# Relative-position bias and softmax: reloads moved to GpSimd's queue, stores to SyncE's, four rows to a chunk

One core of one Trainium2 chip (trn2) runs the kernel. The metric is the time of one execution in device microseconds (us), smaller is better.

## The reference, cut to what matters

```python
def reference(logits, rel_bias):          # logits [2, 8, 2112, 2112] f32, rel_bias [8, 33]
    rel = clip(pos[:, None] - pos[None, :], -16, 16) + 16
    logits = logits + rel_bias[:, rel][None]
    exp = np.exp(logits - logits.max(axis=-1, keepdims=True))
    return exp / exp.sum(axis=-1, keepdims=True)
```

285.5 MB are read and as much is written; each element gets one addition, one exponential and one multiplication.

## The kernel before

Each of 128 partitions owns 264 rows of 2112 elements (8448 bytes). A chunk is 3 rows of every partition, so 88 chunks pass through 8 buffers in SBUF, in place. `F` holds the bias as one strip per partition, built at the start from a small table.

```python
    R = 3                                   # rows of a partition in one chunk
    PARTS = [(0, 2), (2, R)]                # adds and exponentials go in these pieces
    BUFS = 8
    N = T // R                              # 88 chunks
    ...
    def take(eng, sem, v):
        eng.wait_ge(sem, v).then_inc(sem, -v)
    def load(eng, u, start):
        eng.dma_start(out=L[u][:], in_=rows(logits, start)).then_inc(loaded[u], 16)
    def reload(eng, u, start):
        take(eng, stored[u], 16)            # the buffer's store has landed
        load(eng, u, start)
    ...
        @block.sync                         # SyncE: every load
            for c0, c1 in FIRST: ...        # first chunk: four quarter rows, then two rows
            for u in range(1, BUFS):
                if u == BUFS - 1:
                    take(eng, made, 1)      # the last buffer is scratch until the strip is made
                load(eng, u, u * R)
            passes(eng, BUFS, N - 1, lambda u, start: reload(eng, u, start))
        @block.scalar                       # ScalarE: exponentials, and every store
            def whole(u, start):
                exps(eng, u)
                store(eng, u, start)        # waits until VectorE has scaled the chunk
        @block.vector                       # VectorE: the strip, then for each chunk
            ...                             #   bias add, reciprocal of the sums, scaling
```

The softmax here doesn't subtract the row's maximum and nothing guards it: scores larger than these inputs give would overflow.

## Time and profile before

| | before |
|---|---|
| median of 3 runs | 1332.85 us (1332.46 to 1333.08) |
| span of the profiled run | 1331.0 us |
| VectorE, ScalarE busy | 73%, 39% |
| bytes moved, mean rate | 571.0 MB, 429 GB/s |
| DMA packets | 26,501 |
| a load lands after, a store after | 65.9 us, 39.9 us |

To read it: when two transfer queues together fill the DMA engines for nearly the whole span, the time is the bytes plus what is lost at the two ends. The engines' own idle time is then only a consequence. "Lands after" is the median time from the issue of a transfer to its completion; much of it is waiting behind transfers queued earlier.

### The profile page before, as it was taken

The page shows a single profiled execution, that of the slowest core. Times are in us where ns is not written, and L with a number is a line of the kernel's source. Part 1 is how long each engine was busy: PE and PEld are TensorE (multiplying, and loading weights), DVE is VectorE, ACT ScalarE, POOL GpSimd, SP SyncE. Part 2 cuts the span into 40 slices and gives each one's busy share as a digit, 9 for nine tenths or more (in the row PEclk, how much of TensorE's full clock was granted, in tenths as well). Part 3 has the DMA queues.
Part 4 walks back from the last instruction along what each step waited for, and adds up shares of the span by engine and source line. Part 5 has one row for each costly group of instructions (what it writes and reads, how often), then busy time and mean ns, then how long its engine had stood idle before and what let it go on. Part 6 is the DMA issues. An engine that isn't in the chain of part 4 may idle for free. (4 is left out here: it accounts for less than half of the span.)

```text
span 1331.0 us, 3010 instructions
## 1 busy us (share of the span) xinstructions
DVE 968.3 (73%) x627; ACT 524.8 (39%) x529; POOL 0.5 (0%) x6
## 2 busy tenths in 40 slices
DVE  6787867777677777677677777777676776777774
ACT  2535344334433344334433344333443344333441
POOL 0000000000000000000000000000000000000000
DMA  9999999999999999999999999999999999999998
GB/s 374 436 429 436 428 437 428 436 430 436 430 436 429 436 429 436 429 436 430 434 431 434 431 434 431 434 431 433 432 433 431 434 431 434 431 433 431 433 432 347
DMA packets 26501, 571.02 MB, mean 429 GB/s; under 512 B 3072, under 2 KB 3072, under 8 KB 3584
## 3 DMA queue, kind: packets, MB, share of 16 engines
q1 hardware_dynamic: 13536, 285.48, 50.0%
q10 hardware_dynamic: 12960, 285.50, 49.8%
q14 instruction: 5, 0.04, 0.0%
HBM read 285.49 MB, written 285.47 MB: 429 GB/s over the span
## 5 line engine op out<-in xcount | busy, mean ns | idle before, releaser
L125 ACT ACTIVATE L<-L 128x2112 f32<-128x2112 f32 x264 | 515.2, 1952 | 770.3 <-ACTq L88 770.3
L116 DVE TENSOR_TENSOR L<-L,F 128x4224 f32<-128x4224 f32 (+1 forms) x176 | 600.8, 3455 | 137.8 <-DVEq L88 137.7
L143 DVE TENSOR_SCALAR L<-L,tot 128x2112 f32<-128x2112 f32 x264 | 340.5, 1318 | 28.2 <-DVEq L88 6.2
L139 DVE RECIPROCAL tot<-tot 128x2 f32<-128x2 f32 (+1 forms) x176 | 28.3, 161 | 175.5 <-DVEq L88 175.5
L125 ACT ACTIVATION_READ_ACCUMULATOR L<-L 128x1 f32 x264 | 49.2, 186 | 0.0
L125 ACT ACT_TABLE_LOAD x1 | 1.3, 1283 | 18.9 <-ACTq L88 18.9
L187 DVE TENSOR_SCALAR L<-L,rbP 128x71 f32<-128x71 f32 x1 | 0.3, 258 | 3.4 <-DVEq L88 3.4
L195 DVE TENSOR_TENSOR F<-L,rbP 128x2343 f32<-128x2343 f32 x1 | 2.6, 2601 | 0.1
L196 DVE TENSOR_TENSOR F<-F,L 128x2343 f32<-128x2343 f32 x1 | 2.6, 2600 | 0.1
L182 DVE TENSOR_SCALAR L<-L 128x71 int32<-128x71 int32 x1 | 0.2, 198 | 1.5 <-DVEq L88 1.5
L185 DVE TENSOR_SCALAR L<-L 128x71 f32<-128x71 f32 x3 | 0.6, 198 | 0.5 <-DVEq L88 0.2
L190 DVE SCALAR_TENSOR_TENSOR L<-L,rbP 128x71 f32<-128x71 f32 x1 | 0.3, 295 | 0.2 <-DVEq L88 0.2
L183 DVE TENSOR_TENSOR L<-L 128x71 f32<-128x71 int32 x1 | 0.2, 235 | 0.1
L188 DVE COPY F<-rbP 128x16 f32<-128x16 f32 x1 | 0.2, 175 | 0.1
L194 DVE COPY F<-rbP 128x16 f32<-128x16 f32 x1 | 0.2, 174 | 0.1
L246 POOL IOTA L<- 128x71 int32 x1 | 0.2, 189 | 0.0
L243 POOL IOTA L<- 128x71 int32 x1 | 0.2, 188 | 0.6 <-SPq L74 0.6
L290 POOL MEMSET const-uint8-127<- 128x1 uint8 x1 | 0.1, 103 | 0.0
L290 POOL MEMSET const-bfloat16-1.0<- 128x1 bf16 x1 | 0.1, 102 | 0.0
L290 POOL MEMSET const-float32-0.0<- 128x1 f32 x1 | 0.1, 99 | 0.2 <-issue 0.2
L290 POOL MEMSET const-float32-1.0<- 128x1 f32 x1 | 0.1, 98 | 0.0
## 6 DMA issues: line engine op xcount, KB each, us to landing
out_dram<-L ACTq DMA_DIRECT2D x87, 3168.0 KB, 39.9
L<-in_logits_dram SPq DMA_DIRECT2D x86, 3168.0 KB, 65.9
L<-in_logits_dram SPq DMA_DIRECT2D x3, 1056.0 KB, 10.0
L<-in_logits_dram SPq DMA_DIRECT2D x1, 2112.0 KB, 63.2
out_dram<-L ACTq DMA_DIRECT2D x1, 2112.0 KB, 9.6
L<-in_logits_dram SPq DMA_DIRECT2D x4, 264.0 KB, 3.5
out_dram<-L ACTq DMA_DIRECT2D x1, 1056.0 KB, 13.5
rbP<-in_rel_bias_dram ACTq DMA_DIRECT2D x2, 8.2 KB
```

The lines of the kernel that those rows point to most:

```text
L116: eng.tensor_tensor(out=x3, in0=x3, in1=F3, op=ALU.add).then_inc(added, 1)
L125: e = eng.activation(out=x, in_=x, func=EXP, accum_out=tot[u][:, i : i + 1])
L139: eng.reciprocal(out=t, in_=t).then_inc(inverted, 1)
L143: e = eng.tensor_scalar_mul(out=x, in0=x, scalar1=tot[u][:, i : i + 1])
L182: step(eng.tensor_single_scalar(out=qi, in_=qi, scalar=M * Q - 1, op=ALU.bitwise_and))
L183: step(eng.tensor_tensor(out=qm, in0=qi, in1=mm, op=ALU.subtract))
L185: step(eng.tensor_scalar(out=m, in0=qm, scalar1=0.0, scalar2=None, op0=op))
L187: step(eng.tensor_scalar(out=rest, in0=lt, scalar1=low, scalar2=None, op0=ALU.mult))
L190: eng.scalar_tensor_tensor(out=rest, in0=gt, scalar=high, in1=rest, op0=ALU.mult, op1=ALU.add)
L195: step(eng.tensor_tensor(out=blocks, in0=wide(eq), in1=rev, op=ALU.mult))
L196: step(eng.tensor_tensor(out=blocks, in0=blocks, in1=wide(rest), op=ALU.add))
L290: nc = _bacc.Bacc("TRN2", target_bir_lowering=False, num_devices=1)
```

## The change

Its intent: let an otherwise idle engine issue the reloads, take the stores' waits out of ScalarE's stream, make transfers larger, and bring the first chunk in whole rows. The core of the diff:

```diff
-    R = 3
+    R = 4
-    BUFS = 8
+    BUFS = 6
...
         @block.sync
-            for c0, c1 in FIRST: ...
+            for r0, sem in ((0, loaded[0]), (1, late)):   # rows 0 and 2, then rows 1 and 3
+                ...
             for u in range(1, BUFS):
-                load(eng, u, u * R)
-            passes(eng, BUFS, N - 1, lambda u, start: reload(eng, u, start))
+                load(eng, u, u * R, loaded[u])
+            passes(eng, 0, N - 1, lambda u, start, loads: store(eng, u, start))
...
         @block.gpsimd
+            passes(eng, BUFS, N - 1, lambda u, start, loads: reload(eng, u, start))
...
         @block.scalar
-            whole(0, 0)
-            passes(eng, 1, N - 3, whole)
+            exps(eng, 0)
+            passes(eng, 1, N, lambda u, start, loads: exps(eng, u))
```

(Reloads count on semaphores of their own that only grow, so the loops pass the value to wait for; the last chunk is loaded and stored in two pieces.)

More of the change, by code (lines that the diff above doesn't have):

```diff
@@ L64 @@
     mm = mm.bitcast(INT32)
-    FIRST = [(S * m // 4, S * (m + 1) // 4) for m in range(4)]
-    FIRST += [(S * m, S * (m + 1)) for m in range(1, R)]
     def rows(t, start, run=RS):
@@ L75 @@
     loaded = [nc.alloc_semaphore(f"loaded{u}") for u in range(BUFS)]
+    reloaded = [nc.alloc_semaphore(f"reloaded{u}") for u in range(BUFS)]
     stored = [nc.alloc_semaphore(f"stored{u}") for u in range(BUFS)]
@@ L80 @@
     late = nc.alloc_semaphore("late")
+    last = nc.alloc_semaphore("last")
     made = nc.alloc_semaphore("made")
@@ L88, in take, with load @@
         eng.wait_ge(sem, v).then_inc(sem, -v)
-    def load(eng, u, start):
-        eng.dma_start(out=L[u][:], in_=rows(logits, start)).then_inc(loaded[u], 16)
+    def load(eng, u, start, sem):
+        eng.dma_start(out=L[u][:], in_=rows(logits, start)).then_inc(sem, 16)
     def store(eng, u, start, r0=0, r1=R):
@@ L100, in reload @@
         take(eng, stored[u], 16)
-        load(eng, u, start)
+        load(eng, u, start, reloaded[u])
     def add(eng, u, r0, r1, start):
@@ L116, in add, with exps @@
         eng.tensor_tensor(out=x3, in0=x3, in1=F3, op=ALU.add).then_inc(added, 1)
-    def exps(eng, u, first=None):
+    def exps(eng, u):
         for r0, r1 in PARTS:
             take(eng, added, 1)
-            if first and r0 == 0:
-                first()
             for i in range(r0, r1):
@@ L126, in exps, with vec @@
             e.then_inc(summed, 1)
-    def vec(eng, u, start, parts=()):
-        if not parts:
-            take(eng, loaded[u], 16)
-        for m, (r0, r1) in enumerate(PARTS):
-            if parts:
-                take(eng, parts[m], 16)
+    def vec(eng, u, start, loads, parts=False):
+        for (r0, r1), load in zip(PARTS, loads):
+            if load:
+                eng.wait_ge(*load)
             add(eng, u, r0, r1, start)
@@ L147, in passes @@
     def passes(eng, n0, n1, body):
-        k = (n1 - n0) // BUFS * BUFS
-        with eng.Fori(n0 * R, (n0 + k - BUFS) * R + 1, BUFS * R) as i:
-            for u in range(BUFS):
-                body((n0 + u) % BUFS, i + u * R)
-        for n in range(n0 + k, n1):
-            body(n % BUFS, n * R)
+        k = (n1 - n0) // BUFS
+        with eng.Fori(0, (k - 1) * 8 + 1, 8) as i:
+            for m in range(BUFS):
+                n = n0 + m
+                body(n % BUFS, i * (BUFS * R // 8) + n * R, i * 2 + 16 * (n // BUFS))
+        for n in range(n0 + k * BUFS, n1):
+            body(n % BUFS, n * R, 16 * (n // BUFS))
     def strip_of(eng):
@@ L213, in _ @@
         def _(eng):
-            for c0, c1 in FIRST:
+            for r0, sem in ((0, loaded[0]), (1, late)):
+                m = (R - r0 + 1) // 2
+                x = L[0]
                 eng.dma_start(
-                    out=L[0][:, c0:c1],
+                    out=bass.AP(
+                        tensor=x.tensor,
+                        offset=x.offset + r0 * S,
+                        ap=[[list(x.ap[0])[0], P], [2 * S, m], [1, S]],
+                    ),
                     in_=bass.AP(
                         tensor=logits.tensor,
-                        offset=logits.offset + c0,
-                        ap=[[T * S, P], [1, c1 - c0]],
+                        offset=logits.offset + r0 * S,
+                        ap=[[T * S, P], [2 * S, m], [1, S]],
                     ),
-                ).then_inc(loaded[0], 16)
+                ).then_inc(sem, 16)
             for u in range(1, BUFS):
@@ L227, in _ @@
                     take(eng, made, 1)
-                load(eng, u, u * R)
-            passes(eng, BUFS, N - 1, lambda u, start: reload(eng, u, start))
+                load(eng, u, u * R, loaded[u])
+            passes(eng, 0, N - 1, lambda u, start, loads: store(eng, u, start))
             u = (N - 1) % BUFS
-            take(eng, stored[u], 16)
-            for (r0, r1), sem in zip(PARTS, (loaded[u], late)):
-                eng.dma_start(
-                    out=L[u][:, r0 * S : r1 * S],
-                    in_=rows(logits, (N - 1) * R + r0, (r1 - r0) * S),
-                ).then_inc(sem, 16)
+            for r0, r1 in PARTS:
+                store(eng, u, (N - 1) * R, r0, r1)
             for n in range(N - BUFS, N - 1):
@@ L248, in _ @@
             )
+            passes(eng, BUFS, N - 1, lambda u, start, loads: reload(eng, u, start))
+            u = (N - 1) % BUFS
+            take(eng, stored[u], 16)
+            for (r0, r1), sem in zip(PARTS, (reloaded[u], last)):
+                eng.dma_start(
+                    out=L[u][:, r0 * S : r1 * S],
+                    in_=rows(logits, (N - 1) * R + r0, (r1 - r0) * S),
+                ).then_inc(sem, 16)
         @block.scalar
@@ L252, in _ @@
             table_load(eng, range(B))
-            def whole(u, start):
-                exps(eng, u)
-                store(eng, u, start)
-            whole(0, 0)
-            passes(eng, 1, N - 3, whole)
-            u = (N - 3) % BUFS
-            exps(eng, u)
-            exps(eng, (N - 2) % BUFS, lambda: store(eng, u, (N - 3) * R))
-            store(eng, (N - 2) % BUFS, (N - 2) * R)
-            exps(eng, (N - 1) % BUFS)
-            for r0, r1 in PARTS:
-                store(eng, (N - 1) % BUFS, (N - 1) * R, r0, r1)
+            exps(eng, 0)
+            passes(eng, 1, N, lambda u, start, loads: exps(eng, u))
         @block.vector
@@ L271, in _ @@
             strip_of(eng)
-            eng.wait_ge(loaded[0], 16 * len(FIRST)).then_inc(loaded[0], 16 - 16 * len(FIRST))
-            passes(eng, 0, N - 1, lambda u, start: vec(eng, u, start))
+            take(eng, late, 16)
+            for u in range(BUFS):
+                vec(eng, u, u * R, [(loaded[u], 16), None])
+            passes(
+                eng,
+                BUFS,
+                N - 1,
+                lambda u, start, loads: vec(eng, u, start, [(reloaded[u], loads), None]),
+            )
             u = (N - 1) % BUFS
-            vec(eng, u, (N - 1) * R, parts=(loaded[u], late))
+            whole = 16 * ((N - 1) // BUFS)
+            vec(eng, u, (N - 1) * R, [(reloaded[u], whole), (last, 16)], parts=True)
 _INS = ['logits', 'rel_bias']
```

## The prediction

> **What bounds the kernel now.** I began with the page, parts 1 to 3, to see who is full.
>
> ```profile
> span 1331.0 us, 3010 instructions
> DVE 968.3 (73%) x627; ACT 524.8 (39%) x529; POOL 0.5 (0%) x6
> ...
> DMA  9999999999999999999999999999999999999998
> ...
> q1 hardware_dynamic: 13536, 285.48, 50.0%
> q10 hardware_dynamic: 12960, 285.50, 49.8%
> ```
>
> VectorE is at 73%, ScalarE at 39%, while the DMA engines stand at nine tenths or more in all but the last slice. The two queues of part 3, loads (q1, issued by SyncE) and stores (q10, by ScalarE), fill 50.0 + 49.8 = 99.8% of sixteen engines' span. No engine instruction can be the bound; the bytes are.
>
> Next I asked whether the compute engines' waits point the same way (the view of waits, SyncE's queue first: engine and line, what it waited for, us in total, times, longest), and what the DMA queues hold (part 6 of the page: KB each, us from issue to landing):
>
> ```profile
> SPq L88 <- SPq L88: 1276.8, 89, 34.7
> ACT L L125 <- ACTq L88: 770.3, 88, 9.5
> DVE L L116 <- DVEq L88: 137.7, 77, 4.5
> ...
> out_dram<-L ACTq DMA_DIRECT2D x87, 3168.0 KB, 39.9
> L<-in_logits_dram SPq DMA_DIRECT2D x86, 3168.0 KB, 65.9
> ```
>
> VectorE waits 77 times ahead of its bias add, mostly for a load: it is fed, not feeding. A load lands 65.9 us after its issue and a store after 39.9 us. A chunk is 3168 KB each way, so at 432 GB/s a load and a store of it take 2 x 3.244 MB / 432 GB/s = 15.0 us. The 105.8 us in the two queues are thus seven chunk times: there is always work queued. With the 14.6 us from a load's use to its store (VectorE's first add at 14.23 us, the store at 28.87 us) the ring closes: 105.8 + 14.6 = 120.4 = 8 buffers x 15.05 us.
>
> Last, the windows of the two ends, as a saturated kernel can lose time only there (columns: busy time of VectorE, ScalarE, GpSimd, clock, DMA share, GB/s):
>
> ```profile
> 0.00:10.00 10.00, 3.85 (x10) 0.00 (x0) 0.53 (x6) 1.00 0.77 266
> 200.00:600.00 400.00, 292.55 (x187) 156.09 (x158) 0.00 (x0) 1.00 1.00 433
> 1310.00:1320.00 10.00, 5.80 (x6) 2.06 (x2) 0.00 (x0) 1.00 1.00 432
> 1320.00:1331.00 11.00, 0.00 (x0) 0.00 (x0) 0.00 (x0) 1.00 0.42 178
> ```
>
> Against 433 GB/s the first 10 us lose 10 x (433 - 266) / 433 = 3.9 us and the last 11 lose 11 x (433 - 178) / 433 = 6.5 us. Nothing is lost between.
>
> The trace's DMA records give the cost of one descriptor on one engine, the same in both directions: a median 319 ns for 8,448 bytes, 629 ns for 16,896, 940 ns for 25,344. The slope is (940 - 319) ns / 16,896 B, or 27.2 GB/s an engine; what remains is 319 - 310.5 = **8.5 ns for each descriptor**. A completion write takes 9 ns. A chunk gives each engine 8 descriptors (128 partitions over 16 engines), so before needs 88 chunks x 2 x 8 x 940 ns = 1323.5 us of an engine. The span's other 7.5 us are 2.2 us until bytes flow, slow first pieces, completion writes, and a tail in which some engines finish after others.
>
> **What the Trainium skill says.** "DMA: Bandwidth & Descriptors", section "Specifications", puts the ceiling at 435 GB/s, 27.2 for an engine; the slope agrees exactly, and the middle's 433 leaves little. The same page, "Issuing engines are not separate DMA queues", says that DMAs from sync, scalar and gpsimd run on the same 16 engines, so another issuer saves issue time only. An issue here takes 0.34 us (SyncE and ScalarE), 0.34 of each 15 us, and hidden: no gain. "Queues, rings and completion order" says that an engine takes a queue's descriptors in ring order and goes round robin between queues; the equal halves of q1 and q10 fit. "SBUF — State Buffer", section "SBUF: two separate sides", warns that GpSimd writes its descriptors through a port pair that VectorE's two-port operations lock. VectorE's scaling of a row (tensor_scalar, 1318 ns) is about half of a row's add (4.55 us for two), so it does run in such a mode; the kernel before issues no DMA from GpSimd, so the stall itself is in no trace yet.
>
> **The change part by part.**
> 1. *Four rows a chunk.* 66 chunks instead of 88. A descriptor of 33,792 bytes is an estimate from the slope: 1242 + 8.5 = 1250.5 ns. Each engine does 66 x 2 x 8 x 1250.5 ns = 1320.5 us, **3.0 us less**. Completion writes per engine go from 94 loads and 89 stores to 68 and 67: 48 x 9 ns = **0.4 us less**.
> 2. *First and last chunk in pieces.* The first becomes two transfers of whole rows, 512 descriptors of 8,448 bytes where 128 would do: 384 x 8.5 ns / 16 = 0.2 us more. The last in halves, both ways: 0.14 us more. The quarter rows of before go (105 ns on average against 86 typical, 512 of them: 0.6 us), but 512 whole rows at 342 against 319 ns on average bring 0.7 back. Sum: **0.3 us more**.
> 3. *VectorE's work* is the same rows in fewer instructions. One chunk is two adds of 4.55, then the second pair of exponentials (4.15 us from the second add's end to the reciprocal, as in the timeline), a reciprocal and two scalings of 2.85 together: 16.2 us, of a new chunk time of 20.06 us. Before it was 13.15 of 15.05. Slack grows from 1.9 to 3.8 us a chunk. Off the path both times: 0.
> 4. *Stores in SyncE's queue behind its first loads.* The first six chunks, 26 MB, take about 60 us at 436 GB/s. The first store can be issued near 31 us but its descriptors stand behind the loads in the ring, so it runs from about 62 us and the first reload follows at about 72 us (before: 49.1). The engines stay full all the while: loads to 62 us, then stores 0 and 1, already computed. 0 on the time, but the queues change places: with each reload issued as a store ends, about one load is in flight and four stores are queued. The total in both queues should be 6 x 20.06 - 17 = 103 us, now some 20 to 30 us for a load and 75 to 85 for a store.
> 5. *GpSimd as issuer.* 61 reload transfers. A stall behind two scalings (2.6 us) plus some 1 us of generation delays a reload by up to 4 us, while the store queue keeps the engines full: nothing on the path; I allow 0.5 us.
> 6. *The tail.* From the last load to the last store's issue is 11.6 us (add 4.55, exponentials 4.15, scaling 2.85), against 6.8 before. The stores then queued cover it. Ring spread among engines stays: 0.
>
> Sum: -3.0 - 0.4 + 0.3 + 0.5 = -2.6. The measured 1332.85 becomes about **1330 us**.
>
> **The rivals.**
> (a) *GpSimd's descriptors are cut smaller.* Nothing in this trace shows how its generator cuts a run. At 4,096 bytes the loads would have 4,356 descriptors per engine instead of 528, and at 8.5 ns each that adds 3,828 x 8.5 ns = 33 us: about 1363. At 8,448 bytes: 1,584 x 8.5 = 13 us, about 1344. Against it: the sync and scalar queues move 25,344 bytes in one packet.
> (b) *Descriptor starvation empties the engines.* If a reload came later than the four queued stores last, engines would idle. It needs a delay of tens of us against at most a few: VectorE's scalings cover 340.5 of 1331 us and come at most two in a row. An extra 1 us lost on each of 60 reloads would make 1390, but the store queue must be empty for that.
> (c) *The loads' queue gets slower service*, as its descriptors are fetched from SBUF: each engine gives 9 ns more to each of 528 load descriptors: 5 us, 1335.
> (d) *A real gain.* If the ends vanished (3.9 + 6.5 us) the time would fall to about 1320; over 2% faster needs 571 MB in 1306 us, 437 GB/s from the first us to the last, above the ceiling.
>
> **Range and chances.** The 3 us saving comes out of measured descriptor times, and (d) limits luck: low 1324. The upside is skewed by (a) and (c), which the trace cannot exclude: high 1347. Faster by 2% (under 1306) is barred by bytes: 0.01. Slower by 2% (over 1359.5) needs (a) at 4 KB or (b): 0.10. The rest, 0.89.
>
> **What would show it.** Right: DMA at nine tenths throughout, load packets of 33,792 bytes at 1250 ns on a GpSimd queue with about 8,800 packets and some 19,800 packets in all (26,501 before), the first reload near 72 us, loads landing much sooner than stores, VectorE near 957 us busy and idling for loads. Step 4 is wrong if stores still land in about 40 us. Step 5 is wrong if slices of the middle fall under 430 GB/s or GpSimd's issues stand far behind the store that released them. The prediction fails if the packet count stays above 26,501 (rival a), or if the packets of the reloads take longer than their size says (rival c).

## The result

The four runs of the result gave 1362.34, 1329.60, 1331.35 and 1360.91 us, a median of 1346.13; a fifth, taken beside them, gave 1331.38. No run lay near that median: the times fall in **two groups**, near 1330 and near 1361. The kernel before had 1332.46 to 1333.08 in its runs. The ratio of fast runs is 0.9985, with a 95% interval of 0.9965 to 1.0004: no change clear of noise. (A ratio here is the mean of one kernel's fast runs over the mean of the other's of the same rounds, so not quite the ratio of the medians.) A second, longer submission of the same kernel, called "again" below, gave 1334.21, 1336.58, 1330.93, 1332.69, 1330.77 and 1364.26, ratio of fast runs 0.9995. Over both, 3 of 11 runs were slow. The record gives a clock of 1.00 for slow and fast runs alike, so that is not the difference.

The one profile of the first submission is of a slow run, the one of "again" of a fast run. So the fast one is what the prediction is held against. From its page (parts 1 and 3, and part 6: transfer, issuing queue, count, KB each, us to landing):

```profile
span 1331.6 us, 2431 instructions
DVE 954.3 (72%) x539; ACT 529.5 (40%) x529; POOL 33.7 (3%) x67
...
q1 hardware_dynamic: 10912, 311.43, 54.3%
q0 software_dynamic: 8784, 259.53, 45.2%
...
out_dram<-L SPq DMA_DIRECT2D x65, 4224.0 KB, 67.5
L<-in_logits_dram POOLq DMA_DIRECT2D x59, 4224.0 KB, 34.0
```

The queues are again full: 54.3 + 45.2 = 99.5%. GpSimd's queue q0 has 8784 packets, as one run of 33,792 bytes is one packet there too, and the landings have changed places, 34.0 us for a reload and 67.5 for a store. Packets number 19,843 in all.

The slow run's page, the same kernel:

```profile
span 1359.8 us, 2431 instructions
GB/s 394 426 431 426 429 429 420 426 430 426 427 427 424 427 420 419 424 431 422 421 427 423 419 427 419 423 425 419 420 422 416 427 417 419 426 417 422 426 418 291
...
out_dram<-L SPq DMA_DIRECT2D x65, 4224.0 KB, 69.2
L<-in_logits_dram POOLq DMA_DIRECT2D x59, 4224.0 KB, 36.2
```

For comparison, the same line of the kernel before:

```profile
GB/s 374 436 429 436 428 437 428 436 430 436 430 436 429 436 429 436 429 436 430 434 431 434 431 434 431 434 431 433 432 433 431 434 431 434 431 433 431 433 432 347
```

The engines are as busy, but move 416 to 431 GB/s in the slices of the middle, where the kernel before has 428 to 437. The time is lost inside packets. In the trace's DMA records, the reload packets of the slow run take 1300.3 ns on average against 1250.9 for an undisturbed one; at the 99th percentile 2118. There are 7552 of them on 16 engines: (1300.3 - 1250.9) ns x 7552 / 16 = **23.3 us of excess for each engine**. The large packets of SyncE's queue (stores, and the five first loads with 0.7 us of it) add 3.7 us. In the fast run the two together are 1.8 us. That explains 25.1 of the 28.2 us between the two spans; most of the rest is an uneven end, as these windows show, "again" ahead of the slow run (busy VectorE, ScalarE, GpSimd, clock, DMA share, GB/s):

```profile
1310.00:1320.00 10.00, 0.66 (x1) 0.00 (x0) 0.00 (x0) 1.00 0.99 424
1320.00:1330.00 10.00, 0.00 (x0) 0.00 (x0) 0.00 (x0) 1.00 0.27 117
```

```profile
1330.00:1340.00 10.00, 7.15 (x7) 4.00 (x4) 0.00 (x0) 1.00 0.83 355
1340.00:1350.00 10.00, 0.00 (x0) 0.00 (x0) 0.00 (x0) 1.00 0.78 333
1350.00:1360.00 10.00, 0.00 (x0) 0.00 (x0) 0.00 (x0) 1.00 0.29 123
```

After a fast run's full slices, the share falls at once to 0.27; the slow run spends 20 us at 0.83 and 0.78 first, as engines that stalled less have finished.

One line of the view of waits of each, for VectorE's wait on loads ("again", then the slow run: us in total, times, longest):

```profile
DVE L L116 <- DMA L<-in_logits_dram: 222.6, 56, 9.5
```

```profile
DVE L L116 <- DMA L<-in_logits_dram: 250.1, 56, 10.7
```

VectorE waits on loads in both. In the slow one it waits longer because the loads come later; its own busy time is 954.6 us against 954.3.

### The profile page after: what moved, and what is told of

It is laid out like the page before. It is cut to its first block, busy times and chain, and to the rows that moved or that the text cites. A ratio compares the mean times of both kernels' runs of the same rounds, so it can differ in the third digit from the quotient of the medians.

```text
span 1359.8 us, 2431 instructions
## 1 busy us (share of the span) xinstructions
DVE 954.6 (70%) x539; ACT 529.5 (39%) x529; POOL 35.5 (3%) x67
## 2 busy tenths in 40 slices
DMA packets 19843, 571.00 MB, mean 420 GB/s; under 512 B 2304, under 2 KB 2304, under 8 KB 2304
## 3 DMA queue, kind: packets, MB, share of 16 engines
q0 software_dynamic: 8784, 259.53, 45.9%
## 5 line engine op out<-in xcount | busy, mean ns | idle before, releaser
L116 DVE TENSOR_TENSOR L<-L,F 128x4224 f32<-128x4224 f32 x132 | 595.8, 4554 | 250.5 <-DMA L<-in_logits_dram 250.1
L139 DVE TENSOR_SCALAR L<-L,tot 128x2112 f32<-128x2112 f32 x264 | 336.5, 1317 | 20.2 <-DVEq L88 4.3
L135 DVE RECIPROCAL tot<-tot 128x2 f32<-128x2 f32 x132 | 21.4, 162 | 100.6 <-DVEq L88 100.6
L91 POOL DMA_DIRECT2D L<-in_logits_dram x59 | 33.9, 575 | 1222.9 <-POOLq L88 1222.9
L187 DVE TENSOR_SCALAR L<-L,rbP 128x71 f32<-128x71 f32 x1 | 0.3, 259 | 10.1 <-DVEq L88 10.1
L255 POOL DMA_DIRECT2D L<-in_logits_dram x2 | 1.1, 530 | 20.6 <-POOLq L88 20.6
## 6 DMA issues: line engine op xcount, KB each, us to landing
L<-in_logits_dram POOLq DMA_DIRECT2D x59, 4224.0 KB, 36.2
out_dram<-L SPq DMA_DIRECT2D x2, 2112.0 KB, 17.2
```

The costliest lines, as they stand in the source:

```text
L116: eng.tensor_tensor(out=x3, in0=x3, in1=F3, op=ALU.add).then_inc(added, 1)
L135: eng.reciprocal(out=t, in_=t).then_inc(inverted, 1)
L139: e = eng.tensor_scalar_mul(out=x, in0=x, scalar1=tot[u][:, i : i + 1])
L187: step(eng.tensor_scalar(out=rest, in0=lt, scalar1=low, scalar2=None, op0=ALU.mult))
L255: eng.dma_start(out=L[u][:, r0 * S : r1 * S], in_=rows(logits, (N - 1) * R + r0, (r1 - r0) * S),).then_inc(sem, 16)
```

## The experiments

Twelve submissions, the changed kernel once more and eleven others, each beside runs of the kernel before on the same chip (three chips; the kernel before stayed within 1330.94 to 1335.15 us in all 33 of those). The first question was what the slow group belongs to: the software queue, the chunk size, or the way the queues are arranged.

**Run 1, again.** No edit.

> The changed kernel once more, five rounds. Its first five runs fell in two groups, 1329.6 to 1331.4 and 1360.9 to 1362.3 us; the profiled one was slow, and there the reload packets of GpSimd's queue took 1300 ns on average against 1251 typical, 23.3 us of excess per DMA engine, while the store packets had 3.7 us. Theory S (software queue): both groups come again, fast runs near 1330, and if a fast run is profiled its reload packets have under 3 us of excess. Theory N (noise of that one chip): a single group near 1330, and the kernel before scatters as much when this one does.

Measured: the six times above, five near 1331 to 1337 and one of 1364.26. The kernel before did not scatter alongside it. Two groups come back, and the kernel before stays tight beside them, so theory N falls (the record does not name the chip of the first submission); a fast profile has 0.5 us of reload excess per engine, as theory S said.

**Run 2, chunks.** The kernel before with

```diff
-    R = 3
+    R = 4
-    BUFS = 8
+    BUFS = 6
```

> The kernel before with chunks of 4 rows in 6 buffers alone; loads stay on SyncE's queue, stores on ScalarE's. Prediction's step 1 (descriptors): 3.4 us less than before, so 1329.4, with packets of 33,792 bytes at 1251 ns. Theory S: one group of runs, no slow ones, as no packet comes from GpSimd. Theory P (pattern: the stalls come from 4-row transfers of loads and stores meeting in memory): slow runs near 1360 here too, with stalled load packets.

Measured: 1348.50, 1343.24, 1335.41, 1347.66, 1354.22, 1357.99. There is no group near 1331 at all. (The record calls a run slow from 1.5% above the fastest of its kernel, so only the last; the ratio of the other five, 1.0088 with 1.0049 to 1.0127, is still clear of noise.) Its load packets have 6.7 us of excess per engine, on SyncE's queue, with no DMA from GpSimd anywhere. **Theory S falls**: the stalls do not need the software queue. Part of the loss is again in the end, where the records show engines nearly a whole transfer apart (the sixteen completions of a load lie 18.1 us from each other in the median, and some 23 us in the last chunks).

```profile
out_dram<-L ACTq DMA_DIRECT2D x65, 4224.0 KB, 46.2
L<-in_logits_dram SPq DMA_DIRECT2D x64, 4224.0 KB, 57.9
```

**Run 3, queues.** The changed kernel with

```diff
-    R = 4
+    R = 3
-    BUFS = 6
+    BUFS = 8
```

> The changed kernel with chunks of 3 rows in 8 buffers, so the queues and the first chunk's pieces alone. Prediction's steps 2 and 5: about 1333.5 in fast runs (no saving of descriptors, 0.5 us for GpSimd). Theory S: two groups again, the slow one up to 30 us above. Theory P: one group, reload packets of 25,344 bytes at 940 ns with under 1 us of excess per engine, as before.

Measured: 1332.70 to 1335.05 in five runs, median 1333.90, ratio 1.0005 (0.9992 to 1.0018). No stall: reload packets at 940.2 ns on average. Step 5 and step 2 together come to +0.6 us in the medians, which the interval does not tell from 0.

**Run 4, actstores.** The changed kernel with the stores issued by ScalarE:

```diff
         @block.sync
-            passes(eng, 0, N - 1, lambda u, start, loads: store(eng, u, start))
...
         @block.scalar
-            exps(eng, 0)
-            passes(eng, 1, N, lambda u, start, loads: exps(eng, u))
+            def whole(u, start, loads=0):
+                exps(eng, u)
+                store(eng, u, start)
+            whole(0, 0)
+            passes(eng, 1, N - 1, whole)
```

> The changed kernel with its stores issued by ScalarE as before, so that they do not stand behind SyncE's first loads in one ring; reloads stay with GpSimd. Prediction's step 4: no effect on the time of fast runs, 1330, but the landings swap back, loads near 60 us and stores near 40 in place of 36 and 69, and the first reload near 50 us instead of 78. Theory S: slow runs as often as in the changed kernel. Theory B (backlog: stalls come from reloads that start just as they are needed, with under two of them in flight): no slow runs here, as some three reloads are queued.

Measured: 1330.64, 1330.79, 1331.00, 1329.68, 1329.72; ratio 0.9977 (0.9964 to 0.9990). Tight, no stalls (0.2 us of reload excess). The count alone proves little: at 3 slow runs in 11, five clean ones come by luck once in five times.

```profile
out_dram<-L ACTq DMA_DIRECT2D x65, 4224.0 KB, 76.0
L<-in_logits_dram POOLq DMA_DIRECT2D x59, 4224.0 KB, 26.0
```

The expected exchange of landings did not come: a reload lands after 26.0 us and not 60. So theory B falls as well, with even fewer reloads in flight and no slow run. What had moved was the **phase**. A chunk's load and store take 20 us of full engines, and a reload is issued when a store lands. A reload that lands after 36.2 us lands 16.2 us into a chunk time, that is about 3.8 us ahead of the next store; one that lands after 26.0 us lands 6 us into it. As both streams advance alike, I took this offset for constant through a run; it is not quite, as is said below the table. In the slow profile, 723 of the 7552 load packets take over 1400 ns. By the order of their starts, 89% of these are the second to fourth of an engine's eight in a load transfer, mostly while VectorE is not scaling (its scalings cover 4% of the stalled packets' time and 29% of the others'). This is theory F: stalls come where a 4-row load transfer ends a little ahead of a store transfer.

To move the phase and nothing else, GpSimd was held back once, ahead of its first reload:

```diff
+            take(eng, stored[0], 16)
+            for _ in range(COUNT):
+                eng.iota(pause[:], pattern=[[1, 32]], base=0, channel_multiplier=0).then_inc(paused, 1)
+                take(eng, paused, 1)
+            load(eng, 0, BUFS * R, reloaded[0])
-            passes(eng, BUFS, N - 1, lambda u, start, loads: reload(eng, u, start))
+            passes(eng, BUFS + 1, N - 1, lambda u, start, loads: reload(eng, u, start))
```

**Run 5, late5** (the changed kernel, COUNT 20) and **run 6, late2** (COUNT 10).

> The changed kernel, with GpSimd held back by some 5 us (20 small dependent iotas, timed in the trace) ahead of its first reload, nothing else. While it is held the stores have the engines to themselves, so the store stream gains about twice the pause on the loads, and a reload should land some 10 us sooner: 24 us instead of 34 to 36. Theory F (phase: the load packets stall where a load transfer ends 2 to 4 us ahead of a store transfer, as the slow profile has it, landing 36.2 = 20 + 16.2): no slow run among the five or six, 1331 throughout, load excess under 1 us per engine. Theory M (memory placement drawn anew for a run, whatever the phase): slow runs as before, about one in three of the changed kernel's eleven so far.

> The same with half the pause, some 2.5 us: reloads should land at about 29 us, 9 us into the 20 us chunk time. Theory F: no slow run, about 1331. Theory M: slow runs as often as in the changed kernel.

Measured for late2: 1329.69, 1331.98, 1329.24, 1329.54, 1332.77, no slow run, 0.2 us of reload excess. For late5: 1338.78, 1359.77, 1330.56, 1359.04, 1329.15, 1333.48, two slow in six. Both pauses were longer than planned (5.7 and 10.7 us from the first iota to the issue) and they shifted the landings **the other way**, later and not sooner:

```profile
L<-in_logits_dram POOLq DMA_DIRECT2D x59, 4224.0 KB, 43.3
```

```profile
L<-in_logits_dram POOLq DMA_DIRECT2D x59, 4224.0 KB, 54.6
```

The first is late2, the second late5. My reasoning had the sign wrong: stores that run alone land early and release their reloads early, so more reloads stand in the queue. By phase the two are 43.3 - 2 x 20 = 3.3 us and 54.6 - 2 x 20 = 14.6 us into a chunk time. The first is far from the stalling 16.2 and clean, the second close to it and mixed. The theory holds by the landings measured; as written down, the expectation for late5 missed.

**Run 7, act4.** The tight kernel of run 4 with COUNT 18.

> The tight kernel with ScalarE's stores (five runs, 1329.7 to 1331.0, reloads landing after 26.0 us), with a pause of some 4.5 us ahead of its first reload: reloads should land at 26 - 9 = 17 us, the phase that stalled. Theory F: slow runs appear, 1335 to 1360, and load packets stall. Theory M: tight as without the pause, as the addresses and the queues are the same.

Measured: 1359.96, 1355.93, 1332.12, 1362.01, 1362.19, 1359.90. Reloads land after 37.2 us, 17.2 into a chunk time, and the reload excess is 23.8 us per engine.

```profile
GB/s 394 425 431 426 429 427 423 425 429 425 423 422 420 422 434 421 421 421 424 422 431 421 427 424 421 421 429 426 423 426 419 424 423 422 424 416 420 425 420 312
...
L<-in_logits_dram POOLq DMA_DIRECT2D x59, 4224.0 KB, 37.2
```

The rate through the middle is that of the slow run of the changed kernel, 416 to 434 GB/s.

A single pause of 9.3 us near the start turned five of six runs of a kernel with no slow run in five into slow ones, 25 to 32 us over its median. This is the cleanest evidence for the phase: the same addresses, transfers, queues and buffers in both. So theory M (placement in memory, whatever the phase) falls. The two kernels ran on different chips, but late2 stayed clean on the chip of this one. (The phase was hit by luck: the pause was twice the planned one and shifted the other way.)

**Run 8, queues7.** The 3-row kernel of run 3 with COUNT 28.

> The changed queues with chunks of 3 rows in 8 buffers (no stalls, 1332.7 to 1335.1, reloads landing after 26.4 us = 15 + 11.4), with a pause of some 7 us: landing near 12.4 us, a load ending 2 to 3 us ahead of a store. Theory F in its wide form (the phase alone does it): stalled load packets of 25,344 bytes and slow runs. In its narrow form (phase and 4-row transfers together) and in theory M: none, 1334.

Measured: 1332.60 to 1334.81, no stalls. The landing came to 53.1 us, 8.1 into a chunk time of 15, by this measure not the phase that was sought. By the engines' medians (explained under the table) its loads end 1.8 us ahead of a store all through the run, close to the 2.5 to 5 us of most 4-row profiles that stall. So it speaks for the narrow form, without settling it.

**Run 9, fixedin, and run 10, shiftin.** Run 7's kernel, with reloads that read other rows. Their outputs are wrong, which doesn't matter for the times.

```diff
     def reload(eng, u, start):
         take(eng, stored[u], 16)
-        load(eng, u, start, reloaded[u])
+        load(eng, u, 0, reloaded[u])                  # fixedin: always the first chunk's rows
+        load(eng, u, start - BUFS * R, reloaded[u])   # shiftin: 24 rows earlier
```

> The kernel that stalls most (ScalarE's stores and the 4.5 us pause; 5 of 6 runs slow, load packets 25 us of excess per engine) with every reload reading the first chunk's rows again; a wrong result on purpose. Queues, sizes, buffers and the phase stay (reloads landing near 37 us). Theory A (addresses: the reads of a new region of logits meet the writes of another region in memory): the stalls go or change, nearly all runs near 1332. Theory E (the event itself, a load and a store transfer that both begin within 4 us, stalls the engines whatever is read): 4 or more of 6 runs near 1356 to 1362 again.

> The same with every reload reading the rows six chunks (24 rows) earlier than its own; a wrong result on purpose. The addresses move on as in the stalling kernel, but their distance from those being stored differs by 24 x 8448 bytes. Theory A: fewer or no slow runs if the distance matters, slow as before if only moving on matters. Theory E: slow again, 1356 to 1362.

Measured for fixedin: 1355.85, 1363.93, 1363.69, 1329.31, 1364.95, 1329.27, 1334.99, four slow in seven, 14.7 us of reload excess in the slow profile. For shiftin: 1363.13, 1364.97, 1328.99, 1356.44, 1364.13, 1353.76, five slow in six, 22.8 us. The landings, fixedin first:

```profile
L<-in_logits_dram POOLq DMA_DIRECT2D x59, 4224.0 KB, 37.5
```

```profile
L<-in_logits_dram POOLq DMA_DIRECT2D x59, 4224.0 KB, 37.3
```

The stalls survive both changes of the reads' addresses. So they do not follow what is read; theory A falls for the loads' side. Where the stores write was not varied.

**Run 11, pchunks.** Run 2's kernel, with SyncE's first reload held until GpSimd had seen the first store land and run nine iotas.

```diff
         @block.sync
+            take(eng, go, 1)
+            load(eng, 0, BUFS * R)
-            passes(eng, BUFS, N - 1, lambda u, start: reload(eng, u, start))
+            passes(eng, BUFS + 1, N - 1, lambda u, start: reload(eng, u, start))
         @block.gpsimd
+            take(eng, stored[0], 16)
+            ...                             # nine dependent iotas
+            eng.sem_inc(go, 1)
```

> Chunks of 4 rows alone, with SyncE's loads and ScalarE's stores and no DMA from GpSimd (1335 to 1358 in six runs, landing 57.9 = 2 x 20 + 17.9), and a pause of some 4 us ahead of the first reload. By the pauses so far a landing grows by about twice the pause: some 66 us, 6 us into a chunk time. Theory F: all runs within 1329 to 1332, no stalls; so the phase and not the queue was at fault there. Theory M: 1335 to 1358 as without the pause.

Measured: 1329.84, 1342.83, 1333.92, 1347.22, 1362.80, 1341.16. Mixed: a clean fast run has appeared (it is the profiled one, 0.9 us of load excess), but not all. The landing is 56.0 us, not 66: in this kernel loads were still queued when the first store landed, so a pause of 4.8 us gave the stores little to gain (this reason is argued, not tested). Nor did the expectation's rule of twice the pause hold before: act4 had moved by 11.2 us for 9.3. This is the weakest point of the phase as measured by the landing: 16.0 us into a chunk time, and that run was clean. The medians of the sixteen engines' completions put its loads 7.0 us ahead of a store, against mostly 2 to 5 us in the profiles that stall. One engine's last completion, which the landing takes, is a blunt measure.

**Run 12, queues1.** Run 3's kernel with COUNT 2.

> The changed queues with 3 rows in 8 buffers (landing 26.4 = 15 + 11.4, no stalls), with a pause of some 0.8 us: landing near 28, so 13 of 15 us, a load transfer ending 2 us ahead of a store's. The earlier pause of 28 iotas went past this phase. Theory F in its wide form: stalled packets and runs of 1340 to 1360. Narrow form (4-row transfers only): 1333 to 1335, excess under 1 us.

Measured: 1331.12 to 1332.90, no stalls. The landing is 28.2 us, 13.2 of 15, so by this measure a load ends about 2 us ahead of a store. By the engines' medians it ends 3.1 us behind one, so this run decides nothing; queues7 favours the narrow form, which is not proven.

All of the changed kernels in one table (excess is that of one engine's load or reload packets in the profiled run; "ahead" is by how much the median of a reload's sixteen completions precedes that of the next store, as a median over the reloads; "over 1340" is my line between the groups, which counts more runs as slow than the record does in chunks and pchunks):

| kernel | rows | landing | into a chunk time | ahead, us | excess, us | runs over 1340 us |
|---|---|---|---|---|---|---|
| late2 | 4 | 43.3 | 3.3 of 20 | 10.1 | 0.2 | 0 of 5 |
| actstores | 4 | 26.0 | 6.0 of 20 | 7.6 | 0.2 | 0 of 5 |
| again | 4 | 34.0 | 14.0 of 20 | 5.4 | 0.5 | 1 of 6 |
| late5 | 4 | 54.6 | 14.6 of 20 | 8.4 (from 4.8 to 9.9) | 2.5 | 2 of 6 |
| pchunks | 4 | 56.0 | 16.0 of 20 | 7.0 | 0.9 | 4 of 6 |
| changed kernel, first runs | 4 | 36.2 | 16.2 of 20 | 3.4 | 23.3 | 2 of 5 |
| act4 | 4 | 37.2 | 17.2 of 20 | 3.6 | 23.8 | 5 of 6 |
| shiftin | 4 | 37.3 | 17.3 of 20 | 3.4 | 22.8 | 5 of 6 |
| fixedin | 4 | 37.5 | 17.5 of 20 | 3.2 | 14.7 | 4 of 7 |
| chunks | 4 | 57.9 | 17.9 of 20 | 5.0 | 6.7 | 5 of 6 |
| queues7, queues, queues1 | 3 | 53.1, 26.4, 28.2 | 8.1, 11.4, 13.2 of 15 | 1.8, 14.3, 11.9 | under 0.1 | 0 of 15 |

By the landing, kernels at 3 to 6 us have no slow run in 10, those at 14 to 18 have 28 in 48. But the landing also holds how far the engines have drifted apart: in "again" it grows from 31 to 37 us, while its loads stay 5.0 to 5.4 us ahead. The column "ahead" orders the 4-row profiles better: at 3.2 to 3.6 us the excess is 14.7 to 23.8, at 5.0 it is 6.7, at 5.4 it is 0.5, from 7.0 on under 1 (late5 begins at 4.8 and moves away). It also tells the two profiles of the changed kernel apart before the slow one's reload packets stall (the first at 103.9 us): the slow one's first reload, issued at 78.3 us, is 2.7 us ahead, the fast one's, issued at 77.5 us, 5.0. That is one profile of each; the phase of the other runs is not known, and what sets it from run to run was not tested.

## Why the prediction was right or wrong

Within 2% and a little faster is what the fast runs are, by the steps that were written down; the range held the median only because that median lies between two groups. That is luck. **The prediction missed that there are two groups**: it named one time where the kernel has two, and 1361 lies outside its range. In the slow runs its own last sign of failure came true: the reload packets took longer than their size says, 1300 ns against 1251. Its sign "slices under 430 GB/s" tells nothing, as the kernel before has slices of 428.

Three of its small figures are off, without effect: step 3 adds up to 16.1 us and not 16.2; step 2 charges 0.14 us for halves of the last chunk, which the kernel before also moved in two pieces; and the 14.6 us of the ring are those of the first chunk, where a middle one takes 13.3 (add at 1256.79, store at 1270.12).

**Step 1 (descriptors, -3.4)** held as far as it can be told apart. The new packets take 1251 ns, as worked out from the slope. Four rows against three at the same issuer of reloads, runs 4 and 3 of one batch, gives 1330.64 - 1333.90 = -3.3 us (the two differ in the stores' queue too); late2 and queues7, alike but for rows, buffers and pause, give 1329.69 - 1333.56 = -3.9.

**Step 2 (pieces, +0.3)** overlooked a side effect. The small bias table comes in at the same time, and with 8448-byte packets around it instead of quarter rows its wait grew; the timeline of before and of "again" at the strip's first use of it (start, us, what, and the wait in brackets):

```profile
6.58 0.26 DVE L187 TENSOR_SCALAR L<-L,rbP 128x71 f32<-128x71 f32 x1 [3.44 <-DVEq L88]
```

```profile
12.85 0.26 DVE L187 TENSOR_SCALAR L<-L,rbP 128x71 f32<-128x71 f32 x1 [9.56 <-DVEq L88]
```

The strip is 6.3 us late, so the first add starts at 20.04 and not 14.23 us, and the first store is issued at 37.18 us and not near 31. It is not on the path, as loads fill the engines until then, but it moved step 4's numbers.

**Step 3 (VectorE, 0)** held: busy 954 us, foretold 957.

**Step 4 (stores behind loads)** was right in its mechanism and off in size. Landings changed places, to 34.0 and 67.5 us where 20 to 30 and 75 to 85 were foretold; their sum, 101.5, was foretold as 103. The first reload came at 77.5 us and not 72. Its "0 on the time" is **the step that failed**: the arrangement does not cost time itself, but it sets the phase of the two streams, with loads 2.7 to 5.4 us ahead of a store, on the edge of the region in which load packets stall for some 23 us. With the stores in ScalarE's ring no run was slow (0 of 5), and a pause brings slow runs about (5 of 6). So "0" became some 30 us in 3 of 11 runs. Step 4 does not do it alone: four rows without it stall too (run 2), and three rows with it do not (run 3).

**Step 5 (GpSimd, +0.5)** is not contradicted: +0.6 with step 2 in run 3, within noise. The stall behind the shared port, which no trace had shown before, is real. In late2's timeline, an iota of 0.15 us takes 1.22 us while a scaling runs:

```profile
79.42 0.15 POOL L255 IOTA pause<- 128x32 int32 x1 [0.17 <-POOLq L90]
79.57 2.55 DVE L141 TENSOR_SCALAR L<-L,tot 128x2112 f32<-128x2112 f32 x2 [0.15 <-DVEq L90]
79.73 1.22 POOL L255 IOTA pause<- 128x32 int32 x1 [0.16 <-POOLq L90]
81.11 1.06 POOL L255 IOTA pause<- 128x32 int32 x1 [0.16 <-POOLq L90]
```

The "some 1 us of generation" came from no trace; a reload's issue takes 0.53 us typically and up to 1.37 in the slow profile. Neither costs time, as the store queue keeps the engines full.

**Step 6 (tail, 0)** held for fast runs: "again" falls to a share of 0.27 from 1320 us on, as before did to 0.42.

Of the rivals, (a) is refuted by 8784 packets, and (b) by full slices. (c), slower service of the loads, describes the slow runs well, but it is not a property of GpSimd's queue, as (c) had it, nor 9 ns for each packet: run 2 has stalls without that queue, and the fast runs have that queue without the stalls. **What stays open** is what in the memory or the DMA engines stalls in that phase. It does not need GpSimd as issuer (run 2, though with 6.7 us of excess and not 23, and whether the queue adds to it is not known), it does not follow the addresses read (runs 9 and 10), and the scalings do not explain it. Nor do the adds: they cover 45% of the stalled packets' time in act4 and 46% of the others'; in late2 they cover 92% of the time of the second to fourth packets, which do not stall there. Whether the stores' addresses matter, and whether 3-row transfers are safe or only never met the phase, was not settled.

A kernel that beats the one before is run 4's: 1329.68 to 1331.00 us, 0.2% less, with no slow run in five; against the fast runs of the changed kernel (1329.60 to 1336.58) its gain is that it does not scatter. The 0.2% fits the descriptors' saving; it is small, and its safety rests on a phase that nothing in the code holds in place.

## What to carry to other kernels

When a kernel is bound by full DMA queues, look at the durations of single packets and at every run, not at one median: two runs with the same busy share differed by 28 us. The order of issue at the start largely sets how load and store streams lie against each other for the whole run, so a rearrangement that is free by every sum can still choose between fast and slow; try a second arrangement or a shifted start before judging the change. And a check of the larger chunk alone would have blamed the chunk, a check of the queue alone would have found nothing: the pair had to be varied together with the phase.

## What the Trainium skill lacked or had wrong

- "DMA: Bandwidth & Descriptors", section "Issuing engines are not separate DMA queues", says that issuing from several engines only saves issue time. Here the same stores moved from SyncE's ring to ScalarE's had 0 slow runs in 5 against 3 in 11, which may be luck, but a pause of 9.3 us then made it 5 in 6. No page tells of streams that stall by phase.
- The same page, section "Why small descriptors are slow (HBM only)", gives a packet some 3 cycles, and a DMA operation 32 bytes of metadata (one cycle more, by my estimate). The records here fit 8.5 ns for each packet beside its bytes at 27.2 GB/s, which at that page's 850 MHz is 7 cycles, and it still shows at 25,344 bytes: 88 chunks instead of 66 cost 3.3 us (runs 3 and 4).
- The same page, section "SWDGE vs HWDGE vs iDMA", has a packet on GpSimd's path at 4096 bytes or less, "preferably". The records show runs of 33,792 bytes as one packet each, 8784 packets for 259.53 MB (that both mean the same by a packet is not shown).
- "SBUF — State Buffer", section "SBUF: two separate sides", has GpSimd locked out by a two-port VectorE operation. It agrees (0.15 us became 1.22), but its consequence, engines idle for want of descriptors, did not follow here, as the store queue held work: share 1.00 throughout the middle.
- The same page's summary advises some 358 GB/s for transfers between HBM and SBUF; one core alone moved 433 GB/s here, loads and stores together, so that figure, which the page gets by halving a stack's 716 GB/s between two cores, is no limit for a core alone.
